# Input projections by Strassen's scheme in a two-layer transformer kernel: seven block products for eight, in two passes over halves of the contraction

## The chip, the cores and the metric

The kernel runs on one core of a Trainium2 chip. The core has a matrix engine (TensorE, PE in the profile; its weight loads are the row PEld), a vector engine (VectorE, DVE), an engine for activation functions (ScalarE, ACT), a general-purpose engine (GpSimd, POOL) and a queue engine that issues transfers (SyncE, SP). Each engine works through its own instructions in order and waits on semaphores. SBUF is the on-chip memory, PSUM the accumulators of the matmuls: eight banks of 128 x 512 fp32. The metric is the device time of one execution in microseconds; the time of a kernel is the median over its runs.

## The reference

Two layers of a mixer over 512 latent and 256 context tokens of width 2048. Cut to what matters:

```
for l in range(2):
    shift, scale, gate       = split(silu(c)     @ w_mod[l] + b_mod[l], 3)
    shift_c, scale_c, gate_c = split(silu(c_ctx) @ w_mod[l] + b_mod[l], 3)
    n  = rms_norm(h,  g)*(1 + scale)   + shift        # 512 x 2048
    nc = rms_norm(hc, g)*(1 + scale_c) + shift_c      # 256 x 2048
    p, pc = split(n @ w_in[l]), split(nc @ w_in[l])   # 2048 x 7168: 56 blocks of 128 columns
    # 16 heads of width 128 in four groups: A differential, B windowed with a sink,
    # C 2-D neighbourhood, D with normed q and k; latents also see the context's keys
    o  = attention(p, pc);  oc = attention of the context (layer 0 only)
    h  = h  + gate  * rms_norm((o  * silu(p[12]))  @ w_out[l], g2)
    hc = hc + gate_c* rms_norm((oc * silu(pc[12])) @ w_out[l], g2)   # layer 0 only
```

All is fp32. In layer 1 the context needs only keys and values.

## The kernel before

Every fp32 operand of a large matmul is split into a high part (rounded by ACT, `AF.Copy` into fp32r) and a low part (the rest, a subtraction on DVE): `split` (L175), where the rows L179 and L180 of the profile come from. A product is three matmuls, high by high, high by low and low by high: `mm3` (L185, rows L187 to L189).

The input projection treats one block of 128 output columns at a time (`proj_slots`, L565). The normed tokens lie in SBUF as 16 contraction tiles, split (`nh`, `nl` for the latents, `ch`, `cl` for the context). The weights of a block come as four chunks of four contraction tiles, 128 x 512 (`load_one`, L108); `weights_ahead` (L81) loads them, splits them into `wh`, `wl`, two ahead of their use. The weight tile is the stationary operand and the tokens stream, 512 latents and then, four slots later, 256 of the context (`ctx_steps`). A result is taken from its PSUM bank by the block's own function (`qk_block`, `v_block`, `g_block`).

The 16 heads are units in the order A, D, B, C. `plan` lists their blocks: key, value, query, gate (in B and D two heads share key and value). `layer` (L1061) writes the order out by hand: `drive` (L62) walks over the projection slots of one unit and puts in between, spread by weight, the steps of the previous heads (`head_steps`) and the steps of the modulation (`mod_steps`). A step of the softmax (`softmax_steps`, weight 1.5) multiplies queries by keys into the one score buffer (banks 3 and 4), DVE takes the maximum (L846, L876), ACT the exponential (L849, L886); POOL scales the row (L896). Then `value_steps` transposes, splits and multiplies by the values. Delayed pieces run some slots later (`later`, `tick`).

`mod_steps` (L298) works out shift, scale and gate: a 256 KB piece of `w_mod` is loaded, and DVE adds it, times a scalar, to one sum for the latents' condition and one for the context's (L327). Layer 1's shift and scale are made beside layer 0's projections. At the start of layer 0, `prologue` (L434) norms x and makes shift and scale, partly by matmuls (L479) and partly on DVE (L485), chunk by chunk beside the first unit's products. There POOL makes low parts (L100 for weights, L535 for tokens).

`out_phase` (L1114) multiplies by `w_out` in rounds of 512 output columns, first the context's, then the latents', with the last head's steps beside the first round. Between the layers, context products of layer 1 (`ctx_chunk`) run while the last residuals and norms are made.

The transposes of the heads are rows L917 and L784.

Of the kernel before, what the change touches and what calls it, by code (L numbers as in the profile page):

```python
# [10 lines left out]
F32 = mybir.dt.float32  # L11
# [25 lines left out]
GATE = 40  # L37


class Kernel:  # L40
# [37 lines left out]
    def weights_push(self, items):  # L78
        self.wq += items

    def weights_ahead(self):  # L81
        while self.wsplit < len(self.wq) and self.wsplit <= self.wpos + self.look:
            kind, key = self.wq[self.wsplit]
            if self.wsplit >= self.wload:
                if not self.load_one():
                    break
            raw = self.raws.pop(self.wsplit)
            if kind == "og":
                l, s, k = key
                w = raw.shape[1]  # L90
                hi = self.base.tile([P, w], F32R, tag=f"nh{s}_{k}", name=f"nh{s}_{k}")
                lo = self.base.tile([P, w], F32R, tag=f"nl{s}_{k}", name=f"nl{s}_{k}")
                self.og[s, k] = hi, lo
            else:
                hi = self.wp.tile([P, 512], F32R, tag="wh", bufs=4, name="wh")
                lo = self.wp.tile([P, 512], F32R, tag="wl", bufs=4, name="wl")
                self.ws[self.wsplit] = hi, lo
            if self.pool_lo and kind == "in":
                self.nc.scalar.activation(hi, raw, AF.Copy)  # L99
                self.nc.gpsimd.tensor_sub(lo, raw, hi.bitcast(F32))  # L100
            else:
                self.split(hi, lo, raw)
            self.wsplit += 1
        while self.wload < len(self.wq) and self.wload < self.wsplit + 3:
            if not self.load_one():
                break

    def load_one(self):  # L108
        nc, a = self.nc, self.a
        kind, key = self.wq[self.wload]  # L110
        if kind == "og" and key not in self.stored:
            return False
        raw = self.wp.tile([P, 512], F32, tag="wr", bufs=4, name="wr")
# [11 lines left out]
        self.raws[self.wload] = raw  # L125
# [3 lines left out]
    def weight(self):  # L129
        self.weights_ahead()  # L130
        while self.wq[self.wpos][0] == "og":
            self.wpos += 1
            self.weights_ahead()
        w = self.ws.pop(self.wpos)
        self.wpos += 1
        return w

# [16 lines left out]
    def split_to(self, dst, sl, src, scale=None):  # L154
        self.split(dst["h"][:, sl], dst["l"][:, sl], src, scale)
        dst["ready"] = dst.get("ready", 0) + sl.stop - sl.start

    def split_subs(self, dst, sl, src, scale=None):
# [3 lines left out]
        a, b = slice(0, 64), slice(64, P)  # L162
        if "d" not in dst:
            for t, r, o in ((dst["h"], a, b), (dst["l"], b, a)):
                A.activation(t[r, sl], src[r], AF.Copy)
                V.tensor_sub(t[o, sl], src[r], t[r, sl].bitcast(F32))
        else:
            for t, lo, r, o in ((dst["h"], dst["l"], a, b), (dst["d"], dst["m"], b, a)):
                A.activation(t[r, sl], src[r], AF.Copy, scale=scale)
                V.scalar_tensor_tensor(lo[r, sl], src[r], scale, t[r, sl].bitcast(F32), op0=ALU.mult, op1=ALU.subtract)  # L170
                A.activation(t[o, sl], src[r], AF.Copy, scale=scale)
                A.activation(lo[o, sl], lo[r, sl].bitcast(F32), AF.Copy)
        dst["ready"] = dst.get("ready", 0) + sl.stop - sl.start

    def split(self, hi, lo, src, scale=None):  # L175

        nc = self.nc
        if scale is None:
            nc.scalar.activation(hi, src, AF.Copy)  # L179
            nc.vector.tensor_sub(lo, src, hi.bitcast(F32))  # L180
# [4 lines left out]
    def mm3(self, out, lh, ll, rh, rl, start, stop):  # L185
        mm = self.nc.tensor.matmul
        mm(out, lh, rh, start=start, stop=False)  # L187
        mm(out, lh, rl, start=False, stop=False)  # L188
        mm(out, ll, rh, start=False, stop=stop)  # L189

    def run(self):
        tc, nc, a = self.tc, self.nc, self.a
        with ExitStack() as es:
            base = self.base = es.enter_context(tc.tile_pool(name="base", bufs=1))
            self.wp = es.enter_context(tc.tile_pool(name="wp", bufs=1))
            self.mp = es.enter_context(tc.tile_pool(name="mp", bufs=1))
# [5 lines left out]
            self.wq, self.raws, self.ws = [], {}, {}  # L202
            self.wpos = self.wsplit = self.wload = 0
            self.og, self.stored = {}, set()
            self.pool_lo = self.ctx_done = False
# [27 lines left out]
            self.ogd = self.dp.tile([DEPTH, KT, P, TOK], F32, name="ogd")  # L233
            self.plan()
            self.layer(0, self.prologue)

    def plan(self):

        self.units = []
        for h in range(4):  # L240
            self.units.append(("A", h, h, [("k", KA + h), ("v", VA + h), ("q", QA + h), ("g", GATE + h)]))
        for kind, q0, k0, v0, g0 in (("D", QD, KD, VD, 12), ("B", QB, KB, VB, 4)):
            for h in range(4):
                kv = [("k", k0 + h // 2), ("v", v0 + h // 2)] if h % 2 == 0 else []
                self.units.append((kind, h, g0 + h, kv + [("q", q0 + h), ("g", GATE + g0 + h)]))
        for h in range(4):
            self.units.append(("C", h, 8 + h, [("k", KC + h), ("v", VC + h), ("q", QC + h), ("g", GATE + 8 + h)]))
        self.order = [u[2] for u in self.units]
        for l in range(DEPTH):
            first = [b for _, b in self.units[0][3][:3]]  # L250
            if l > 0:
                for u in self.units[:2]:
                    for _, b in u[3][:2]:
                        self.weights_push([("in", (l, b, c)) for c in range(4)])
            self.weights_push([("in", (l, b, c)) for c in range(4) for b in first])
            for n, u in enumerate(self.units):
                for _, b in u[3][0 if n else 3:]:
                    self.weights_push([("in", (l, b, c)) for c in range(4)])
            for s in ((1, 0) if l < DEPTH - 1 else (0,)):
                for r in range(2 if s else 4):  # L260
                    for k in self.order:
                        if r == 0 and k != self.order[-1]:
                            self.weights_push([("og", (l, s, k))])
                        self.weights_push([("out", (l, k, c)) for c in ((2 * r, 2 * r + 1) if s else (r,))])


    def mod_columns(self, l, kind, c4, ps):
# [5 lines left out]
        if kind == 2:  # L273
# [7 lines left out]
            def turn():  # L281
                tp = self.tbank()[0:4 * ns, 0:P]
                nc.tensor.transpose(tp, t, self.ident)
                rows = self.x3()[0:4 * ns, 0:P]
# [13 lines left out]
    def mod_steps(self, jobs):  # L298
# [13 lines left out]
        def step(i):  # L312
# [22 lines left out]
    def mod_finish(self, job, accs, fold=True):  # L335
# [11 lines left out]
        if ns == 2:  # L347
            t, col = self.x3(), self.halves
# [69 lines left out]
    def make_n(self, l, stream, k, tiles, pool, t):  # L418

        nc = self.nc  # L420
        w = len(tiles) * P
        his, los = (self.nh, self.nl) if stream == 0 else (self.ch, self.cl)
        for i, ht in enumerate(tiles):
            nc.tensor.transpose(t[:, i * P:(i + 1) * P], ht[:, k * P:(k + 1) * P], self.ident)
        hi = self.base.tile([P, w], F32R, tag=f"nh{stream}_{k}", name=f"nh{stream}_{k}")
        lo = self.base.tile([P, w], F32R, tag=f"nl{stream}_{k}", name=f"nl{stream}_{k}")
        full = pool.tile([P, 512], F32, tag="full", bufs=2, name="full")[:, 0:w]
        mA, mB = self.mA[:, l, stream, k:k + 1], self.mB[:, l, stream, k:k + 1]
        nc.scalar.activation(hi, t[:, 0:w], AF.Identity, scale=mA, bias=mB)
        nc.vector.tensor_scalar(full, t[:, 0:w], mA, mB, op0=ALU.mult, op1=ALU.add)  # L430
        nc.vector.tensor_sub(lo, full, hi.bitcast(F32))
        his[k], los[k] = hi, lo

    def prologue(self, blocks):  # L434

        tc, nc, a = self.tc, self.nc, self.a
        self.nh, self.nl, self.ch, self.cl = ([None] * KT for _ in range(4))
        parts = ((0, SEQ), (SEQ, TOK))
        with tc.tile_pool(name="pro", bufs=1, reuse_waits="tile") as pool:
            raws, xs, accs = {}, [], {}  # L440
            seq = [(c4, kind, kk) for c4 in range(4) for kk in range(8) for kind in (1, 0)]
            self.np = 0

            def load(upto):
                while self.np < min(upto, len(seq)):
                    c4, kind, kk = seq[self.np]
                    raw = raws[seq[self.np]] = pool.tile([P, 2, 512], F32, tag="mr", bufs=8, name="mr")
                    col0 = kind * D + c4 * 512
                    nc.sync.dma_start(raw, a["w_mod"][0, kk * 256:(kk + 1) * 256, col0:col0 + 512].rearrange("(k p) c -> p k c", p=P))
                    self.np += 1  # L450

            def load_x(upto):
                while len(xs) < upto:
                    t = pool.tile([P, TOK], F32, tag="x", bufs=KT, name="x")
                    nc.sync.dma_start(t, a["xt"][len(xs)])
                    xs.append(t)

            load(2)
            load_x(KT)
            load(8)  # L460
            tot = [self.mp.tile([P, 512], F32, tag="macc", bufs=2, name="tot")[:, 0:w1 - w0] for w0, w1 in parts]

            def squares(k):
                for t, (w0, w1) in zip(tot, parts):
                    if k == 0:
                        nc.scalar.activation(t, xs[k][:, w0:w1], AF.Square)
                        continue
                    sq = self.mp.tile([P, 512], F32, tag="mraw", bufs=3, name="sq")[:, 0:w1 - w0]
# [911 lines left out]
```

## Time and profile before

| | |
|---|---|
| median of 3 runs (lowest, highest) | 2792.03 us (2788.14, 2792.82) |
| profiled execution: time, span | 2796.49 us, 2794.7 us |
| PE, PEld busy | 2693.9 us (96%), 2234.6 us (80%) |
| DVE, ACT, POOL busy | 1751.9 us (63%), 1045.1 us (37%), 313.2 us (11%) |
| moved by DMA | 331.24 MB, mean 119 GB/s |
| granted clock of TensorE, mean | 0.986 |

A row of the profile's groups reads: line, engine, operation, output <- inputs, shapes, count | busy us, mean ns of one | idle time before it and what ended it. PE counts matmuls as busy from issue to the modelled end, so overlapped ones have durations that add up to more than their time.

### The profile page before, as it was taken

What the parts mean: (1) busy time and instruction counts of PE and PEld (TensorE: products, weight loads), DVE (VectorE), ACT (ScalarE), POOL (GpSimd) and SP (SyncE); (2) the same over time, 40 slices, a digit from 0 to 9 for tenths busy, and PEclk for the clock granted to TensorE, in tenths of its full rate; (3) what the DMA queues carried; (4) which work ended last, traced back from release to release, by engine and by line L of the source; (5) the groups of instructions that cost most, each with busy time, mean ns of one, the idle gap of its engine ahead of it and who ended that gap; (6) DMA issues with size and microseconds to landing.
All of it is one profiled execution on the core that took longest, in us unless ns stands there. A gap on an engine that the chain in (4) does not pass through costs nothing. (4 is left out here: it accounts for less than half of the span.)

```text
span 2794.7 us, 38989 instructions
## 1 busy us (share of the span) xinstructions
PE 2693.9 (96%) x14348; PEld 2234.6 (80%) x14348; DVE 1751.9 (63%) x3399; ACT 1045.1 (37%) x2087; POOL 313.2 (11%) x266
## 2 busy tenths in 40 slices
PE   6989999999999999999999989999999999999997
PEld 1468888888888888888778777888888788888885
DVE  6886988876974746664564577666755644334524
ACT  3334444433333333333553255444433333333422
POOL 1530000011111101010010030000001111000001
PEclk8999999999999999999999989999999999999998
DMA  8841323232431414443763542112312322222533
GB/s 313 279 136 61 119 82 115 86 121 75 152 116 59 125 59 128 126 129 93 222 219 113 184 164 87 61 61 95 111 58 68 128 71 76 81 81 89 177 113 106
DMA packets 178642, 331.24 MB, mean 119 GB/s; under 512 B 20833, under 2 KB 24209, under 8 KB 177937
## 3 DMA queue, kind: packets, MB, share of 16 engines
q1 hardware_dynamic: 178448, 328.74, 36.5%
q8 instruction: 112, 1.84, 0.3%
q14 instruction: 82, 0.66, 0.1%
HBM read 310.42 MB, written 18.24 MB: 118 GB/s over the span
## 5 line engine op out<-in xcount | busy, mean ns | idle before, releaser
L187 PE MATMUL ps<-nh,wh 128*128 128x512 f32 (+1 forms) x3072 | 1079.2, 352 | 11.1 <-ACT wh L99 7.9
L188 PE MATMUL ps<-nl,wh 128*128 128x512 f32 (+1 forms) x3072 | 1065.8, 347 | 5.3 <-POOL nl L535 5.2
L189 PE MATMUL ps<-nh,wl 128*128 128x512 f32 (+1 forms) x3072 | 1066.1, 347 | 4.6 <-POOL wl L100 4.6
L180 DVE TENSOR_TENSOR wl<-wr,wh 128x512 fp32r<-128x512 f32 x624 | 450.0, 723 | 554.9 <-ACT wh L179 537.6
L179 ACT ACTIVATE wh<-wr 128x512 fp32r<-128x512 f32 x624 | 392.7, 630 | 905.2 <-PE ps L188 478.3
L187 PEld LDWEIGHTS ps<-nh,wh 128*128 128x128 f32 x3072 | 582.0, 190 | 92.0 <-issue 10.0
L189 PEld LDWEIGHTS ps<-nh,wl 128*128 128x128 f32 x3072 | 580.7, 189 | 80.4 <-POOL wl L100 6.1
L188 PEld LDWEIGHTS ps<-nl,wh 128*128 128x128 f32 x3072 | 582.0, 189 | 73.8 <-POOL nl L535 9.3
L327 DVE SCALAR_TENSOR_TENSOR macc<-mraw,sc,macc 128x512 f32<-128x512 f32 x420 | 309.8, 771 | 50.4 <-DMA mraw<-in_w_mod 49.9
L188 PE MATMUL ps<-wl,nh 128*128 128x512 f32 x600 | 239.5, 399 | 6.0 <-DVE wl L180 5.9
L187 PE MATMUL ps<-wh,nh 128*128 128x512 f32 x600 | 238.5, 398 | 0.1
L189 PE MATMUL ps<-wh,nl 128*128 128x512 f32 x600 | 238.2, 397 | 0.0
L180 DVE TENSOR_TENSOR PTl<-ps,PTh 128x512 fp32r<-128x512 f32 (+2 forms) x224 | 132.6, 592 | 108.7 <-ACT PTh L179 108.4
L896 POOL TENSOR_SCALAR P<-P,small 128x768 f32<-128x768 f32 (+2 forms) x96 | 97.5, 1015 | 835.7 <-DVE small L895 742.4
L179 ACT ACTIVATE PTh<-ps 128x512 fp32r<-128x512 f32 (+2 forms) x224 | 115.8, 518 | 162.4 <-PE ps L917 155.8
L650 POOL TENSOR_TENSOR rt<-rt 128x512 f32<-128x512 f32 x40 | 62.1, 1552 | 967.8 <-DVE rt L647 967.8
L188 PEld LDWEIGHTS ps<-wl,nh 128*128 128x128 f32 x600 | 113.3, 189 | 36.7 <-DVE wl L180 10.5
L187 PEld LDWEIGHTS ps<-wh,nh 128*128 128x128 f32 x600 | 113.3, 189 | 27.8 <-ACT wh L179 1.0
L189 PEld LDWEIGHTS ps<-wh,nl 128*128 128x128 f32 x600 | 113.5, 189 | 27.0
L917 PE MATMUL ps<-ident,P 128*128 128x128 f32 x672 | 105.2, 272 | 1.4 <-DVE PTl L180 1.3
L917 PEld LDWEIGHTS ps<-ident,P 128*128 128x128 f32 x672 | 83.5, 140 | 24.1 <-DVE PTl L180 1.8
L876 DVE TENSOR_REDUCE small<-ps 128x1 f32<-128x768 f32 (+3 forms) x120 | 88.8, 740 | 11.4 <-PE ps L189 7.4
(232 smaller groups left out, 2882.6 us busy)
## 6 DMA issues: line engine op xcount, KB each, us to landing
wr<-in_w_in SPq DMA_DIRECT2D x464, 256.0 KB, 3.0
mraw<-in_w_mod SPq DMA_DIRECT2D x256, 256.0 KB, 3.0
wr<-in_w_out SPq DMA_DIRECT2D x192, 256.0 KB, 3.3
mr<-in_w_mod SPq DMA_DIRECT2D x64, 512.0 KB, 5.3
wr<-ogd SPq DMA_DIRECT2D x30, 256.0 KB, 2.7
x<-in_xt SPq DMA_DIRECT2D x16, 384.0 KB, 7.8
ogd<-g SPq DMA_DIRECT2D x15, 384.0 KB, 2.7
h<-in_x SPq DMA_DIRECT2D x16, 256.0 KB, 4.9
```

Of the source, the lines that this page charges most:

```text
L179: nc.scalar.activation(hi, src, AF.Copy)
L180: nc.vector.tensor_sub(lo, src, hi.bitcast(F32))
L187: mm(out, lh, rh, start=start, stop=False)
L188: mm(out, lh, rl, start=False, stop=False)
L189: mm(out, ll, rh, start=False, stop=stop)
L327: nc.vector.scalar_tensor_tensor(acc, raw, col, acc, op0=ALU.mult, op1=ALU.add)
L650: nc.gpsimd.tensor_add(t1, t1, t2)
L876: nc.vector.reduce_max(nm, sv, axis=AX, negate=True)
L896: nc.gpsimd.tensor_scalar(Pt, Pt, sm, 0.5, op0=ALU.mult, op1=ALU.mult)
L917: nc.tensor.transpose(T[:, i * P:(i + 1) * P], st["P", t][:, c:c + P], self.ident)
```

## The change

Two blocks make a pair: (key, value) or (query, gate). Tokens are kept in two halves of 384 (256 latents and 128 of the context each). A pass takes half of the contraction, 8 of the 16 tiles, again in two halves of four. So a pass is a 2 x 2 by 2 x 2 block product, and Winograd's form of Strassen's scheme makes it from seven products, numbered 1 to 7, in the order 1, 6, 2, 5, 7, 3, 4, accumulated in three PSUM banks (`CHAIN`).

- Weights: POOL forms the sums s1 and s2 and two differences of a pair's four chunks in each pass (`sums`, `split_product`), then ACT and DVE split seven operands. In the second pass the low parts for products 5 and 7 are made by POOL.
- Tokens: the seven token operands of a pass, split, stay in one area of SBUF (`arena`); `reload` writes them for the first pair of a pass, or after the last pair of the pass before. The output phase keeps its gated heads in the same area.
- Results: ACT copies product 1 out of PSUM; the others are added to it by DVE as they end. The first pass writes the sums of all 56 blocks to DRAM (`part`), the second one fetches them a pair ahead (`hold_parts`), POOL adds product 1 to three quarters of them, and DVE the rest.
- Order: a layer is now first pass over all 28 pairs, with only modulation and the second half's token work beside it, and then the second pass over all 28 pairs, with all heads' steps beside it, at a density set by `goal`. The block functions read the result from SBUF, not from PSUM.
- Layer 0's prologue makes only the first halves of shift and scale, by matmuls, before the first pair. The rest and the gate (128 steps) run beside the first pass. Layer 1's shift and scale (128 steps) run beside the latents' rounds of layer 0's output phase; its gate (64 steps, one stream) beside its first pass.
- In `mod_steps` the context's stream is made by ACT (product) and POOL (sum) and not by DVE.
- The context products between the layers (`ctx_chunk`) go; the context's normed tokens pass through DRAM (`cnd`).

```
+    def sums(self, g):
+        if g["sums"] or not all(self.need(g, i) for i in range(3)):
+            return g["sums"]
+        add = self.nc.gpsimd
...
+        add.tensor_add(g["s1"], g[1], g[2])
+        add.tensor_sub(g["s2"], g["s1"], g[0])
+        add.tensor_sub(g[1], g[0], g[1])
...
+    def split_product(self, g, n):
...
+        src = {1: 0, 6: "s2", 2: 3, 5: "s1", 7: 1, 3: 3, 4: 2}[n]
+        hi, lo = self.new_pair()
+        self.split(hi, lo, g[src], pool=n in self.pool_lo)
+        if n == 2:
+            self.nc.gpsimd.tensor_sub(g[3], g[3], g["s2"])
...
             for acc, s in zip(accs[j], streams):
                 col = self.sc[:, k, s:s + 1]
+                if s == 1:
+                    t = acc if k == 0 else self.mp.tile([P, 512], F32, tag="mt", bufs=2, name="mt")
+                    nc.scalar.activation(t, raw, AF.Copy, scale=col)
+                    if k:
+                        nc.gpsimd.tensor_add(acc, acc, t)
+                    continue
...
+    def pair_slots(self, l, s, n, i, hooks=None):
...
+        def slot(m, half):
+            if half == 0:
+                for fn in before.get(m, ()):
+                    fn()
+                r["w"] = self.weight()
+            hi, lo = r["w"]
+            th, tl = self.operand(m)
+            out = self.bank(CHAIN[m], w)
+            for j in (2 * half, 2 * half + 1):
+                js = slice(j * P, (j + 1) * P)
+                self.mm3(out, hi[:, js], lo[:, js], th[:, j, 0:w], tl[:, j, 0:w], m in FIRST and j == 0, m in LAST and j == 3, True)
+            if half:
+                read(m, out)
...
+        def read(m, ps):
+            V = nc.vector
+            if m == 1:
+                r["c"] = tiles()
...
+                nc.scalar.activation(r["s"], ps, AF.Copy)
+                if s:
+                    for c, h in ((r["c"][1], 0), (r["c"][1], 1), (r["c"][0], 1)):
+                        nc.gpsimd.tensor_add(c[:, h], c[:, h], r["s"])
...
+                c = {6: c2[:, 0], 4: c2[:, 0], 5: c2[:, 1], 7: c2[:, 1], 3: c1[:, 1]}[m]
+                V.tensor_add(c, ps, c if s or m in (7, 4) else s1)
...
+                    nc.sync.dma_start(self.part[l, b, :, :, 0:w], c)
...
+        self.drive(slots[0])
...
+        self.drive([x for s in slots[1:-1] for x in s], self.late)
+        self.drive(slots[-1])
...
+        self.pool_lo = (5, 7)
+        steps, left, last = [], 0, 0
+        for n, (kind, h, gh, prs) in enumerate(self.units):
...
+            goal = left - last * (0 if n == len(self.units) - 1 else 0.3 if len(prs) > 1 else 0.7)
...
+            self.drive([x for i in range(len(prs)) for x in self.pair_slots(l, 1, n, i)], now)
```

A query/gate pair of layer 1 has only the latents, 256 a half.

More of the change, by code (lines that the diff above doesn't have):

```diff
@@ L98, in weights_ahead @@
[L98 to L102, printed above, removed]
+            kind, g, key = self.wq[self.wsplit]
+            if not (self.split_product(g, key) if kind == "st" else self.split_one(kind, g, key)):
+                break
             self.wsplit += 1
-        while self.wload < len(self.wq) and self.wload < self.wsplit + 3:
+        while self.load_one():
+            pass
@@ new lines, in reload, with step, reloads @@
+    def reload(self, n, ns, ts, pool=()):
+        hi, lo = self.operand(n)
+        def step(j):
+            if n in (1, 2, 3):
+                src = ns[j + (0 if n == 1 else 4)][:, int(n == 3)]
+            else:
+                src = ts[j][{5: 0, 7: 0, 6: 1, 4: 1}[n]]
+            self.split(hi[:, j], lo[:, j], src, pool=j in pool)
+        return [lambda j=j: step(j) for j in range(4)]
+    def reloads(self, ns, ts, pool=()):
+        out = {n: self.reload(n, ns, ts, pool) for n in ORDER}
+        out[6] += self.token_sums(ns, ts, 4, True)
+        out[5] += self.token_sums(ns, ts, 3, True)
+        return out
@@ L629, in x3, with hold_parts @@
+    def hold_parts(self):
+        if not self.to_hold:
+            return
+        l, blocks, w = self.to_hold.pop(0)
+        out = []
+        for _, b in blocks:
+            c = self.cp.tile([P, 2, HT], F32, tag="c", bufs=4, name="c")[:, :, 0:w]
+            self.nc.sync.dma_start(c, self.part[l, b, :, :, 0:w])
+            out.append(c)
+        self.held.append(out)
     def x3(self):
@@ L1057, in unit_blocks, with layer @@
             else:
-                out.append(self.g_block(l, b, dst))
-        return out
-    def layer(self, l, start):
+                fn = self.g_block(l, b, dst)
+            self.take[n, what] = fn
+    def layer(self, l):
         tc, nc, a = self.tc, self.nc, self.a
-        sts = {}
-        blocks = {n: self.unit_blocks(l, n, sts) for n in range(len(self.units))}
-        start(blocks[0])
+        pairs = [(n, i) for n, u in enumerate(self.units) for i in range(len(u[3]))]
+        self.tbanks, self.tb = [5, 6], 0
+        before = {m: self.first[ORDER[i + 1]] if i + 1 < len(ORDER) else [] for i, m in enumerate(ORDER)}
+        before[ORDER[0]] = self.first[ORDER[0]] + before[ORDER[0]]
+        again = self.reloads(self.ns2, self.ts2)
+        slots = []
+        for p in pairs:
+            hooks = (before, {}) if p == pairs[0] else ({}, again) if p == pairs[-1] else None
+            slots.append(self.pair_slots(l, 0, *p, hooks))
+        self.drive(slots[0])
@@ L1107, in layer @@
-        self.ctx_steps()
-        self.pend = None
+        self.take, sts = {}, {}
+        for n in range(len(self.units)):
+            self.unit_blocks(l, n, sts)
+        self.held = []
+        self.to_hold = []
+        for n, i in pairs:
+            blocks = self.units[n][3][i]
+            wide = l < DEPTH - 1 or blocks[0][0] == "k"
+            self.to_hold.append((l, blocks, HT if wide else 2 * P))
+        self.hold_parts()
+        self.pool_lo = (5, 7)
+        steps, left, last = [], 0, 0
```

745 lines of the change are left out of this document (386 added, 359 removed).

## The prediction

> **What bounds the kernel now.** I read the totals on the page first, then the chain that ended last, then the groups of instructions by shape, then single rows in order of time.
>
> ```profile
> span 2794.7 us, 38989 instructions
> PE 2693.9 (96%) x14348; PEld 2234.6 (80%) x14348; DVE 1751.9 (63%) x3399; ACT 1045.1 (37%) x2087; POOL 313.2 (11%) x266
> PE   6989999999999999999999989999999999999997
> PE 34%; DVE 2%; ACT 1%; DMA 0%; issue 0%; POOL 0%; DVEq 0%; POOLq 0%
> ```
>
> TensorE works through the whole span but for the start, the seam between the layers and the end, and it leads the chain of waits. Its busy time counts overlapped matmuls, so the price of one is taken from the distance between starts:
>
> ```profile
> 872.82 0.34 PE L188 MATMUL ps<-PTl,vh 128*128 128x384 f32 x1
> 873.00 0.34 PE L189 MATMUL ps<-PTh,vl 128*128 128x384 f32 x1
> ...
> 1141.76 0.39 PE L187 MATMUL ps<-nh,wh 128*128 128x512 f32 x1
> 1141.99 0.39 PE L188 MATMUL ps<-nl,wh 128*128 128x512 f32 x1
> ...
> 1142.56 0.28 PE L188 MATMUL ps<-nl,wh 128*128 128x256 f32 x1
> 1142.68 0.28 PE L189 MATMUL ps<-nh,wl 128*128 128x256 f32 x1
> ```
>
> A 512-wide matmul takes 0.2325 us (mean over a longer run of such starts; 0.23 here), a 256-wide 0.118, a 384-wide 0.1745. The counts:
>
> ```profile
> L187 PE MATMUL ps<-nh,wh 128*128 128x512 f32 x1792 | 717.7, 401 | 2.0 <-ACT wh L99 1.6 <-DVE mB L292 0.4
> L187 PE MATMUL ps<-nh,wh 128*128 128x256 f32 x1280 | 362.6, 283 | 9.1 <-ACT wh L99 6.3 <-DVE kl L166 2.9
> L187 PE MATMUL ps<-wh,nh 128*128 128x512 f32 x600 | 238.5, 398 | 0.1
> L917 PE MATMUL ps<-ident,P 128*128 128x128 f32 x672 | 105.2, 272 | 1.4 <-DVE PTl L180 1.3
> L187 PE MATMUL ps<-PTh,vh 128*128 128x512 f32 x128 | 59.7, 466 | 0.0
> L187 PE MATMUL ps<-kh,qh 128*128 128x256 f32 x152 | 43.7, 287 | 0.8 <-ACT Pc L886 0.6 <-ACT P L886 0.2
> ```
>
> Each row stands three times (L187, L188, L189). Projections: 3 × (1792 × 0.2325 + 1280 × 0.118) = 1703 us, 61% of the span. Output: 1920 (with 40 on the last head's tiles) × 0.2325 = 446. Attention, by the same widths and all its counts, about 396: 208 in layer 0, 188 in layer 1.
>
> **The change, term by term.** *Matmuls.* A pair of output blocks costs 7 products × 4 contraction tiles × 3 = 84 matmuls in each of two passes, 384 wide, or 256 wide for the 16 query/gate pairs of layer 1: 40 × 168 × 0.1745 + 16 × 168 × 0.118 = 1490. TensorE sheds 213 us. One wide pair in one pass is then 14.7 us, a narrow one 9.9.
>
> *What is paid for it.* Weight tiles to split go from 8 to 14 a pair; POOL forms four sums of 128x512 a pair and pass, all of SBUF operands; five or six reads of PSUM a pair and pass replace one or two; layer 0's second stream of the modulation moves from DVE to ACT and a POOL add; all heads move into the second pass; layer 1's modulation moves from layer 0's projections to its output phase. Prices:
>
> ```profile
> L327 DVE SCALAR_TENSOR_TENSOR macc<-mraw,sc,macc 128x512 f32<-128x512 f32 x420 | 309.8, 771 | 50.4 <-DMA mraw<-in_w_mod 49.9
> L180 DVE TENSOR_TENSOR wl<-wr,wh 128x512 fp32r<-128x512 f32 x624 | 450.0, 723 | 554.9 <-ACT wh L179 537.6 <-PE ps L917 5.6 <-PE ps L784 4.6
> L180 DVE TENSOR_TENSOR PTl<-ps,PTh 128x384 fp32r<-128x384 f32 x32 | 17.7, 554 | 11.9 <-ACT PTh L179 11.9
> 118.00 5.82 POOL L100 TENSOR_TENSOR wl<-wr,wh 128x512 fp32r<-128x512 f32 x1 [6.47 <-ACT wh L99]
> 119.29 3.39 DVE L485 SCALAR_TENSOR_TENSOR macc<-mr,sc,macc 128x512 f32<-128x512 f32 x5
> 126.24 1.27 POOL L100 TENSOR_TENSOR wl<-wr,wh 128x512 fp32r<-128x512 f32 x1 [2.42 <-ACT wh L99]
> 171.50 5.73 POOL L535 TENSOR_TENSOR nl<-x,nh 128x256 fp32r<-128x256 f32 x4
> 172.01 5.77 DVE L327 SCALAR_TENSOR_TENSOR macc<-mraw,sc,macc 128x512 f32<-128x512 f32 x4
> ```
>
> The last five rows matter most. DVE alone runs five 512-wide operations in 3.39 us, 0.66 each; a POOL subtraction that takes 1.27 alone lasted 5.82 while DVE did so. Where both are queued, four DVE and four POOL operations (two 512 wide, two 256) take 5.7 us, not the 2.7 of DVE alone: they take turns. Four times 0.66 from 5.73 leaves 3.09 for POOL, so 1.03 for a 512-wide one. DVE and POOL operations with two SBUF operands add up, 1.69 us for one of each. The subtraction from PSUM keeps its price beside POOL, so only the SBUF ones count.
>
> The Trainium skill (SBUF — State Buffer, Who interferes with whom) says that a DVE instruction with two SBUF inputs and a GpSimd instruction that reads SBUF block each other, the second until the first has finished. With POOL's whole 1.27 a turn would cost 1.93, and the 256 turns below 61 us more than in my sum; the trace agrees on the blocking, and its 1.69 a turn is used.
>
> *By stage* (span of the profiled execution, 2794.7 us; its time is 2796.5, 4.5 above the median of the three runs):
>
> ```profile
> mr<-in_w_mod SPq DMA_DIRECT2D x64, 512.0 KB, 5.3
> 0.00:100.00 100.00, 75.87 (x227) 27.84 (x228) 74.46 (x135) 35.81 (x71) 24.18 (x21) 0.88 0.87 304
> 300.00:600.00 300.00, 296.12 (x1759) 256.57 (x1758) 255.95 (x578) 121.85 (x254) 20.26 (x13) 1.00 0.35 108
> 1000.00:1200.00 200.00, 200.00 (x1212) 177.70 (x1212) 116.51 (x220) 65.22 (x138) 21.63 (x24) 1.00 0.35 109
> 1610.00:1630.00 20.00, 16.25 (x98) 14.54 (x97) 16.85 (x33) 12.29 (x32) 8.87 (x7) 0.84 0.63 221
> 1800.00:2200.00 400.00, 395.79 (x2120) 335.42 (x2119) 246.32 (x504) 155.36 (x287) 31.61 (x27) 1.00 0.25 80
> ```
>
> (These are windows: PE, PEld, DVE, ACT, POOL busy, granted clock, DMA share, GB/s.)
>
> 1. Start: only the first halves of scale and shift (16.8 MB, 32 of the 512 KB loads) and x (6.3 MB) stand ahead of the first product: 77 us at 304 GB/s, 23 for what cannot overlap (statistics before the first matmuls, modulation, operand splits). 100.
> 2. Layer 0, first pass: TensorE needs 28 × 14.7 = 410. The shared turn needs 28 × (4 × 1.03 + 7 × 0.66) = 245 for weights and 128 modulation steps × 1.69 = 216: 461. DVE's stalls hold its weight splits, those hold TensorE. 480 (ends: 425, if turns hide; 540, if the PSUM reads never overlap POOL).
> 3. Hand-over of operands, twice: 28 splits on ACT and DVE in one pair's time: 10 each (0 to 20).
> 4. Layer 0, second pass: matmuls 410 + 208 = 618. Some 394 weighted head steps now fall into 392 slots of six matmuls (1.05 us), twice as dense as before. One buffer holds the scores, so the next scores wait for this chain:
>
> ```profile
> 1850.30 0.40 PE L822 MATMUL ps<-kh,qh 128*128 128x512 f32 x1
> 1851.21 0.96 DVE L846 TENSOR_REDUCE small<-ps 128x1 f32<-128x768 f32 x1 [1.00 <-PE ps L823]
> 1852.21 0.90 ACT L849 ACTIVATE P<-ps,small 128x768 f32<-128x768 f32 x1 [2.83 <-DVE small L846]
> L886 ACT ACTIVATE P<-ps,small,rs 128x768 f32<-128x768 f32 x32 | 31.7, 990 | 46.7 <-DVE small L883 42.3 <-DVE rs L400 2.6 <-PE ps L189 1.9
> L876 DVE TENSOR_REDUCE small<-ps 128x1 f32<-128x640 f32 x32 | 26.3, 820 | 2.1
> ```
>
> 2.81 us from the first score to the end of the exponential in group A, by the other rows about 3.5 in D and 3.0 to 3.5 in B and C. Available are 1.4 slots (1.45 us) plus the scores' own 0.7 to 1.06: 2.05 to 2.5. The difference over 32 + 16 + 32 latent steps is 65 us. Before, the slots of these steps took over 3 us, which is why windows like 1000 to 1200 show no idle time. Waiting behind other DVE work is not in that row (0.01 us there); before, DVE was 58 to 85% busy with most of it, now its own work is about 83% (of its 1752 us, 310 and 450 are the modulation and weight rows above, some 430 of the rest layer 0's heads; 28 pairs × (5 × 0.66 + 6 × 0.5) = 176 more; 606 of 728), with POOL's turns on top: between 0 and 1 us a step, 0.4 taken, 45 for 120 steps. 728.
> 5. Output of layer 0: context rounds 384 × 0.2325 = 89, plus the 16 of idle time they have now. Latent rounds: matmuls 179, but 128 × 1.69 for the modulation, 64 + 15 + 8 operations of 0.66: 273; 280 taken. Sum 385.
> 6. Seam: the row at 1610 shows it; now nothing fills the tail (15 us for residual and second norm), then 8 × 1.3 us on ACT for the new operands, the first splits and a cooled clock: 40. Before, 20 us of context products lay there.
> 7. Layer 1, first pass: 12 × 14.7 + 16 × 9.9 = 335; a narrow pair also needs 8.7 of shared turns and 1.5 of modulation, just over its 9.9. 345 (335 to 365).
> 8. Layer 1, second pass: 335 + 188 = 523, chain 44 by the same comparison, 30 for DVE waits (80 steps × 0.4). 597.
> 9. Output of layer 1: 768 × 0.2325 = 179 and the 24 of today's tail. 203.
>
> Sum: 100 + 480 + 20 + 728 + 385 + 40 + 345 + 597 + 203 = 2898, 101 above the profiled execution's time with its 1.8 us around the span; 2893 against the median, rounded to **2890**. In short: 213 us of matmuls and some 70 of today's start and small stalls are won, and spent on turns (70 + 101), stalls in dense heads (184) and hand-overs. The sums in DRAM go by SP's queue:
>
> ```profile
> DMA packets 178642, 331.24 MB, mean 119 GB/s; under 512 B 20833, under 2 KB 24209, under 8 KB 177937
> wr<-in_w_in SPq DMA_DIRECT2D x464, 256.0 KB, 3.0
> ```
>
> 22 MB written and read again in layer 0, less in layer 1, beside 331 MB at 119 GB/s where the start shows 304: costed at nothing, covered by their being fetched one pair (14.7 us) ahead; uncovered, 3.0 us of landing a pair, 84 a layer.
>
> **Rivals.** *Faster: turns and waits hide.* If a modulation step costs under (410 − 245) / 128 = 1.3 us of shared time, pass one is bound by matmuls, and under 1.0 the output rounds are too: then 55 and 95 us go, with half the DVE waits 2705. For it: 50 to 60% use of each engine. Against: the rows at 171 us. If the softmax chains hid too, 2560, which needs a second score buffer that isn't there.
> *Slower still: POOL late.* In second passes POOL makes the low parts for products 5 and 7. POOL stands in order behind the scaling of P, which waits for a reciprocal that stands on DVE behind the next step's maximum. What queues behind: the low parts and the next pair's sums, needed two products (4.2 us, narrow 2.8) later. 2 us lost a pair is 112: 3005. Turns that hold POOL's whole 1.27 would end on the way there, 2950, and share this chance; the four and four in 5.7 us speak against it. That length is what the Trainium skill's section named above would make of it.
> *No change:* with the smallest of my terms (no DVE waits, 461 and 273 bare, no hand-over, 335, a seam of 33) the sum is 2760; DVE waits of 0.1 us a step and half the hand-overs bring it to 2790, where gain and losses meet.
>
> **How the numbers follow.** Forecast 0.48, POOL late 0.15, no change 0.05, turns hide 0.26, all hides 0.06. Slower by over 0.2% (what a measurement here can tell) 0.63, same 0.05, faster 0.32. The likeliest case alone spans 2810 to 2960; the range 2670 to 3000 leaves out full hiding and the upper half of POOL late.
>
> **What would show it.** Right: in layer 0's first pass DVE operations with two SBUF operands over 1.2 us beside a POOL busy above 60%; idle TensorE waiting for `wl`; in second passes TensorE waiting on ACT P; latent output rounds over 250 us. Wrong: 384-wide products back to back at 0.175 us through pass one, DVE durations of 0.7 beside POOL, output rounds near 185.

## The result: 19% slower, where 3.5% was forecast

The changed kernel takes 3314.01 us (median of 4 runs, 3310.43 to 3314.50) against 2792.16: ratio 1.187, 95% interval 1.1849 to 1.189. The direction was forecast, the size was not: 522 us lost for 98, and the time lies 314 above the end of the range. The profiled execution took 3314.17 us. From the page of the changed kernel: totals, the DVE, POOL and clock lines of the 40 slices; and from its view of cores:

```profile
span 3312.4 us, 43903 instructions
PE 2728.5 (82%) x14488; PEld 2415.7 (73%) x14488; DVE 2583.7 (78%) x4076; ACT 1484.5 (45%) x2900; POOL 1652.1 (50%) x1230
DVE  4988769889989877766898987788788788776634
POOL 0776547664335455551366645543554355566301
PEclk8788898989888999999998869999889898989999
...
core 0: 3312.4 us, clock 0.905
```

TensorE was 96% busy before and is 82% now; no engine is near full over the whole span, so they wait for each other. The granted clock fell from 0.986 to 0.905. The stages, as windows (PE, PEld, DVE, ACT, POOL busy, granted clock, DMA share, GB/s): layer 0's first pass, its second, its output with the seam, layer 1's first pass, its second.

```profile
91.20:684.30 593.10, 473.33 (x2427) 454.66 (x2426) 492.71 (x562) 273.80 (x473) 389.77 (x257) 0.89 0.44 143
684.30:1513.20 828.90, 703.01 (x3798) 633.78 (x3797) 676.19 (x1321) 379.05 (x829) 421.38 (x347) 0.92 0.24 76
1513.20:1951.40 438.20, 326.71 (x1350) 254.12 (x1348) 378.49 (x503) 237.23 (x451) 210.54 (x141) 0.86 0.66 209
1951.40:2357.80 406.40, 369.27 (x2431) 361.73 (x2430) 324.64 (x437) 173.49 (x324) 202.77 (x137) 0.94 0.47 154
2357.80:3105.00 747.20, 601.76 (x3511) 545.47 (x3510) 579.90 (x1022) 327.78 (x657) 403.89 (x327) 0.90 0.24 76
```

Set against the forecast, with the distances between the starts of all matmuls in the trace split into three: what the matmul takes at full clock, what it takes more without waiting (half clock), and waits. The split rests on how a lengthened distance is assigned; other rules give 190 to 240 us of half clock and 660 to 710 of waits.

| stage | forecast | measured | full clock | half clock | waits |
|---|---|---|---|---|---|
| start | 100 | 91 | 58 | 2 | 24 |
| layer 0, first pass | 480 | 593 | 419 | 38 | 136 |
| layer 0, second pass, hand-over | 738 | 829 | 616 | 58 | 155 |
| output 0 and seam | 425 | 438 | 291 | 27 | 120 |
| layer 1, first pass | 345 | 406 | 341 | 21 | 44 |
| layer 1, second pass, hand-over | 607 | 747 | 505 | 71 | 171 |
| output 1 | 203 | 207 | 187 | 1 | 2 |
| sum | 2898 | 3312 | 2417 | 218 | 652 |

(The other 25 us lie ahead of the first matmul and behind the last.)

What TensorE waited for, over the whole span (total us, times, longest):

```profile
PE ps L284 <- DVE c L762: 123.6, 63, 5.7
PE ps L460 <- DVE fold L455: 66.3, 6, 29.6
PE ps L1071 <- POOL P L1050: 47.8, 23, 5.2
PE ps L284 <- ACT s L750: 46.1, 14, 7.4
PE ps L285 <- DVE PTl L276: 41.6, 27, 5.4
...
PE ps L976 <- ACT P L1003: 23.1, 16, 3.5
PE ps L285 <- DVE wl L276: 22.4, 13, 7.6
PE ps L284 <- ACT P L1040: 18.2, 22, 2.7
...
PE ps L286 <- DVE wl L276: 13.1, 9, 4.0
PE ps L286 <- POOL wl L276: 11.9, 4, 4.2
```

The largest wait is for the reads of PSUM (`c`, 124 us), not for weight splits (`wl`, 47 in three rows). The groups of the first pass of layer 0 (busy us, mean ns, idle before):

```profile
L429 DVE SCALAR_TENSOR_TENSOR macc<-mraw,sc,macc 128x512 f32<-128x512 f32 x120 | 155.1, 1292 | 3.0 <-DMA mraw<-in_w_mod 1.7
L276 DVE TENSOR_TENSOR wl<-wr,wh 128x512 fp32r<-128x512 f32 x139 | 151.4, 1091 | 41.3 <-ACT wh L275 41.0 <-PE ps L286 0.2
L762 DVE TENSOR_TENSOR c<-ps,s 128x384 f32<-128x384 f32 x84 | 46.2, 550 | 22.4 <-PE ps L286 22.2
...
L424 POOL TENSOR_TENSOR macc<-macc,mt 128x512 f32<-128x512 f32 x120 | 185.4, 1545 | 93.2 <-ACT mt L422 85.6 <-ACT macc L422 4.4 <-DMA mraw<-in_w_mod 0.8
...
L422 ACT ACTIVATE mt<-mraw,sc 128x512 f32<-128x512 f32 x120 | 86.6, 723 | 149.0 <-POOL macc L424 125.7 <-DMA mraw<-in_w_mod 21.2 <-PE ps L460 1.6
```

A read of PSUM itself kept its 0.55 us. What made it late is what stands ahead of it in DVE's order, as rows of the timeline show (start, us, operation):

```profile
568.78 6.67 POOL L424 TENSOR_TENSOR macc<-macc,mt 128x512 f32<-128x512 f32 x4
569.18 1.77 DVE L276 TENSOR_TENSOR wl<-wr,wh 128x512 fp32r<-128x512 f32 x1
570.45 0.72 ACT L422 ACTIVATE mt<-mraw,sc 128x512 f32<-128x512 f32 x1 [0.75 <-POOL macc L424]
570.87 0.54 DVE L762 TENSOR_TENSOR c<-ps,s 128x384 f32<-128x384 f32 x1
...
571.56 0.41 PE L284 MATMUL ps<-arena,wh 128*128 128x384 f32 x1 [1.61 <-DVE c L762]
...
572.55 1.78 DVE L429 SCALAR_TENSOR_TENSOR macc<-mraw,sc,macc 128x512 f32<-128x512 f32 x1
...
575.93 0.68 DVE L276 TENSOR_TENSOR wl<-s,wh 128x512 fp32r<-128x512 f32 x1
```

Beside POOL, DVE's operations take 1.77 and 1.78 us; a split of the same shape once POOL is done, at 575.93, takes 0.68. The read of PSUM stands behind the first of them, and the matmul at 571.56 has waited 1.61 us for it.

### The profile page after: what moved, and what is told of

The parts are those of the page before. It is cut to its first block, busy times and chain, and to the rows that moved or that the text cites. A ratio compares the mean times of both kernels' runs of the same rounds, so it can differ in the third digit from the quotient of the medians.

```text
span 3312.4 us, 43903 instructions
## 1 busy us (share of the span) xinstructions
PE 2728.5 (82%) x14488; PEld 2415.7 (73%) x14488; DVE 2583.7 (78%) x4076; ACT 1484.5 (45%) x2900; POOL 1652.1 (50%) x1230
## 5 line engine op out<-in xcount | busy, mean ns | idle before, releaser
L284 PE MATMUL ps<-arena,wh 128*128 128x384 f32 (+1 forms) x3136 | 1078.9, 344 | 181.0 <-DVE c L762 123.1
L286 PE MATMUL ps<-arena,wl 128*128 128x384 f32 (+1 forms) x3136 | 1058.0, 338 | 25.2 <-DVE wl L276 13.1
L285 PE MATMUL ps<-arena,wh 128*128 128x384 f32 (+1 forms) x3136 | 1060.7, 338 | 10.4 <-POOL arena L276 6.0
L276 DVE TENSOR_TENSOR wl<-wr,wh 128x512 fp32r<-128x512 f32 x696 | 629.5, 908 | 209.1 <-ACT wh L275 198.6
L284 PEld LDWEIGHTS ps<-arena,wh 128*128 128x128 f32 x3136 | 634.8, 202 | 212.0 <-DVE c L762 92.2
L286 PEld LDWEIGHTS ps<-arena,wl 128*128 128x128 f32 x3136 | 634.1, 202 | 32.2 <-DVE wl L276 16.6
L285 PEld LDWEIGHTS ps<-arena,wh 128*128 128x128 f32 x3136 | 635.3, 203 | 18.3 <-POOL arena L276 9.1
L424 POOL TENSOR_TENSOR macc<-macc,mt 128x512 f32<-128x512 f32 x240 | 373.3, 1556 | 267.8 <-ACT mt L422 243.2
L762 DVE TENSOR_TENSOR c<-ps,c 128x384 f32<-128x384 f32 (+1 forms) x392 | 201.2, 514 | 136.8 <-PE ps L286 83.1
L285 PE MATMUL ps<-wl,arena 128*128 128x512 f32 x640 | 261.3, 408 | 22.7 <-DVE wl L276 22.4
L284 PE MATMUL ps<-wh,arena 128*128 128x512 f32 x640 | 260.9, 408 | 3.1 <-ACT cn L526 2.3
L286 PE MATMUL ps<-wh,arena 128*128 128x512 f32 x640 | 259.0, 405 | 0.0
L149 POOL TENSOR_TENSOR s<-wr 128x512 f32<-128x512 f32 x112 | 174.2, 1555 | 80.7 <-DMA wr<-in_w_in 57.7
```

The lines of the kernel that those rows point to most:

```text
L149: add.tensor_add(g["s1"], g[1], g[2])
L276: (nc.gpsimd if pool else nc.vector).tensor_sub(lo, src, hi.bitcast(F32))
L284: mm(out, lh, rh, start=start, stop=False, skip_group_check=parts)
L285: mm(out, lh, rl, start=False, stop=False, skip_group_check=parts)
L286: mm(out, ll, rh, start=False, stop=stop, skip_group_check=parts)
L424: nc.gpsimd.tensor_add(acc, acc, t)
```

## The experiments

### What each part of POOL's new work costs

Theory: POOL's operations slow DVE, and through DVE's, ACT's and TensorE's orders the whole. So each kind was moved to DVE, alone and then all together. The modulation's second stream (the branch with ACT's product and POOL's addition is never taken, so both streams are made by DVE):

```
-                if s == 1:
+                if False:
```

> The changed kernel with both streams of the modulation on DVE again; POOL keeps the weight sums, the low parts of products 5 and 7 and the additions of the first pass's sums. Theory (POOL's share of the modulation takes turns with DVE, ACT waits for POOL with weight splits queued behind it, and TensorE falls to half clock): layer 0's first pass falls from 593 us to 430-490, output and seam of layer 0 from 438 to about 385, the second passes stay within 20 us; total 3060 to 3180. Rival (DVE is simply full, and POOL's share relieves it): 128 operations of 0.66 us come to DVE in each of the two places, total 3350 to 3480.

3214.72 us, ratio 1.1516 (1.1498 to 1.1533): 99 less than the changed kernel. The direction fits, the size is under the theory's: layer 0's first pass fell to 538, not to 430 to 490, which leaves more to the other kinds. The weight sums:

```
-        add = self.nc.gpsimd
+        add = self.nc.vector
-            self.nc.gpsimd.tensor_sub(g[3], g[3], g["s2"])
+            self.nc.vector.tensor_sub(g[3], g[3], g["s2"])
```

> The changed kernel, with only the four weight sums and differences of a pair (128x512, SBUF operands) on DVE instead of POOL: 56 pairs and passes, 224 operations. The modulation's second stream, the additions of first parts and the low parts of products 5 and 7 stay on POOL. Moving the modulation alone won 99 us and moving all of POOL's new work 374. Theory (every POOL operation on SBUF holds up the DVE operations beside it and through them TensorE, so each kind counts by its number): 120 to 200 us faster than the changed kernel's 3314, 3115 to 3195, with something won in each of the four passes. Rival (what counts is only where POOL stands in order in the second passes): under 60 us, all but none of it in the first passes.

3115.63 us, ratio 1.1148 (1.1124 to 1.1172): 198 less, at the fast end of the theory, with something won in all four passes. (The operations are 448, 56 pairs in two passes by four; 224 was a miscount.) The first parts and the low parts:

```
-                        nc.gpsimd.tensor_add(c[:, h], c[:, h], r["s"])
+                        nc.vector.tensor_add(c[:, h], c[:, h], r["s"])
-        self.pool_lo = (5, 7)
+        self.pool_lo = ()
```

> The changed kernel, with the additions of the first parts (three of 128x384 or 128x256 a pair, second passes only) and the low parts of products 5 and 7 on DVE instead of POOL; the weight sums and the modulation's second stream stay on POOL. With the heads left out the second passes still waited 215 us for DVE's reads of PSUM, which need what POOL added. Rival of the prediction, POOL late: the second passes shrink by 110 us or more together (829 to under 770, 747 to under 695) and nothing else moves; 3140 to 3200. Theory that every POOL operation counts by its number: 168 additions and 56 low parts, the same count as the weight sums and in a shorter time, 80 to 150 us, also only in the second passes; so this run and the one with the sums on DVE should add up, with the modulation's 99, to about the 374 of all three. If they add to much less, the parts cover for each other.

3200.41 us, ratio 1.146 (1.1442 to 1.1477): 114 less, nearly all in the second passes, 53 in each. (The operations are 280: 168 additions and 112 low parts, not 56.) That lies inside the theory and just short of what the rival asked for, and both put it into the second passes, so the run does not tell them apart. The trace of the changed kernel shows how much is lateness alone: DVE waited 51 us for POOL's additions to the parts, TensorE 12 for POOL's low parts. The three edits together:

> The changed kernel with all that POOL was given on DVE: both modulation streams, the four weight sums of a pair and pass, the low parts of products 5 and 7, the additions of the first pass's sums. POOL is left with what it did before. Theory (taking turns costs more than the work itself): DVE alone needs 16.3 us a pair in layer 0's first pass: 460 to 480 us there, second passes 750 to 800 and 660 to 700, total 2990 to 3150. Rival (DVE load is what counts): every stage gets longer than in the changed kernel, total above 3400.

2940.25 us, ratio 1.0534 (1.0515 to 1.0554): 374 less, faster than expected. The parts add to 411, so they overlap by 37. Moving an operation takes away three things at once: what it adds to DVE's operations beside it, the waits for POOL itself, and in the modulation a product on ACT. Stages, in us:

| stage | changed | modulation | sums | parts | all |
|---|---|---|---|---|---|
| layer 0, first pass | 593 | 538 | 544 | 590 | 470 |
| layer 0, second pass | 829 | 827 | 777 | 776 | 754 |
| output 0 and seam | 438 | 393 | 431 | 440 | 395 |
| layer 1, first pass | 406 | 406 | 376 | 405 | 377 |
| layer 1, second pass | 747 | 750 | 691 | 694 | 646 |

The page's totals with all on DVE, and four of its groups:

```profile
PE 2608.4 (89%) x14488; PEld 2306.3 (79%) x14488; DVE 2553.8 (87%) x5060; ACT 1325.7 (45%) x2644; POOL 299.4 (10%) x262
...
L276 DVE TENSOR_TENSOR wl<-wr,wh 128x512 fp32r<-128x512 f32 x752 | 531.3, 708 | 139.1 <-ACT wh L275 135.5
L429 DVE SCALAR_TENSOR_TENSOR macc<-mraw,sc,macc 128x512 f32<-128x512 f32 x540 | 390.2, 757 | 21.0 <-DMA mraw<-in_w_mod 20.3
...
L149 DVE TENSOR_TENSOR s<-wr 128x512 f32<-128x512 f32 x112 | 76.5, 683 | 3.9 <-issue 1.3 <-DMA lt<-in_lam 1.3 <-DMA wr<-in_w_in 0.9
...
L753 DVE TENSOR_TENSOR c<-c,s 128x384 f32<-128x384 f32 x120 | 71.1, 630 | 0.3
```

The most telling pair of numbers: DVE took over 984 operations (4076 to 5060), and its busy time fell, from 2583.7 to 2553.8 us. What POOL had relieved DVE of had come back in full as longer DVE operations.

### The same move in the kernel before

The kernel before with the context's modulation stream as ACT product and POOL addition:

```
+                if s == 1:
+                    t = acc if k == 0 else raw
+                    nc.scalar.activation(t, raw, AF.Copy, scale=col)
+                    if k:
+                        nc.gpsimd.tensor_add(acc, acc, t)
+                    continue
```

> The kernel before with one part of the change alone: the context's modulation stream is scaled by ACT (in place in the loaded piece) and summed by POOL, 192 steps in layer 0's projections and none elsewhere. Theory: DVE sheds 127 us there, but 192 turns of 1.03 us come in; where TensorE had slack it costs little: 2800 to 2880. Rival (POOL's work beside DVE is free): DVE is relieved and the time stays at 2785 to 2795.

2880.44 us, ratio 1.0317 (1.03 to 1.0334), the theory's upper end: 88 us lost by this move alone, in a kernel with no Strassen and room on DVE. Its 192 products on ACT are part of the move: ACT waited 117 us for DVE to be done with the piece that it scales in place, and TensorE's waits for the exponentials grew from 11 to 38 us. How the 88 divide was not tested.

### Is it ACT's place behind POOL?

The same in two places, cut to the argument that changes:

```
-  tag="mt", bufs=2
+  tag="mt", bufs=3 if self.mp is self.ph else 2
```

> The changed kernel with three buffers instead of two for the modulation's product that ACT makes and POOL adds, in layer 0's stage only (there is no room for it in the output phase). In the first pass of layer 0 ACT waited 126 us for POOL to free such a buffer, with the copies of weights for TensorE behind it in its order, while DVE was idle a sixth of the time. Theory (the pass is long because ACT stands behind POOL, and not because the turns fill it): the pass falls from 593 by 20 to 60 us, and ACT's wait for POOL by half; 3255 to 3295. Rival (the turns set the rate: POOL and DVE share one port, a deeper buffer only moves where the waiting is): the pass stays within 10 us of 593; 3304 to 3324.

3300.42 us, ratio 1.1828 (1.1808 to 1.1848). The pass shrank by 11 us, between the two expectations. ACT's wait for POOL fell from 126 to 89, TensorE's for ACT `s` from 39 to 25, but its wait for DVE `c` rose from 67 to 75. ACT's place is a small part; mostly the waiting moved.

### Dense heads, or the second pass itself?

The changed kernel without scores, softmax and values (each head keeps only its last step):

> The changed kernel without scores, softmax and values: a head ends right after its projections and the gate alone is stored, so the attention is left out. Theory (the heads beside the second pass are too dense for DVE and POOL in order): the second passes fall from 829 and 747 us to about 480 and 390, near the 410 and 335 of their matmuls; total about 2610. Rival (the second pass is slow by itself, by POOL's additions and low parts): they stay above 600 and 520, total above 2860. First passes and output unchanged under both.

2868.61 us in one run, as the rival said. Its two second passes:

```profile
683.00:1284.20 601.20, 482.98 (x2506) 462.43 (x2505) 475.55 (x682) 227.63 (x440) 374.52 (x272) 0.91 0.30 100
2110.20:2670.10 559.90, 419.49 (x2492) 405.38 (x2491) 424.34 (x606) 209.90 (x390) 359.12 (x274) 0.87 0.29 97
```

They still took 601 and 560 us, though their matmuls at full clock are 428 and 349: 173 and 211 lost with no head in them, 202 of it waits of TensorE for DVE `c`. The theory that dense heads cause the loss fell. With heads, the passes take 228 and 187 more, of which 188 and 156 are matmuls: dense heads cost 40 + 31 us beyond their matmuls. The same with all of POOL's new work on DVE:

> The kernel with all of POOL's new work on DVE, and the heads' scores, softmax and values left out (finish alone stays), so the second passes hold the projections, their parts and what the heads leave to set up. With POOL burdened the same passes without heads took 601 and 560 us, against 428 and 349 of matmuls. Theory (POOL's work is what slows the second pass by itself): 430 to 480 and 350 to 400, the whole 2500 to 2600. Rival (a second pass waits because a part is needed two products after it is fetched, whoever adds it): over 560 and over 500.

2451.33 us in one run, and windows of its two second passes:

```profile
559.60:1057.50 497.90, 450.88 (x2507) 437.86 (x2506) 470.87 (x936) 234.07 (x446) 35.68 (x25) 0.96 0.37 121
1798.40:2252.90 454.50, 388.63 (x2491) 375.88 (x2490) 434.89 (x854) 211.18 (x387) 36.92 (x26) 0.93 0.37 118
```

498 and 455, both over the theory's 430 to 480 and 350 to 400; the first lies far under the rival's 560, the second halfway between 400 and the rival's 500. (The total, 2451, is under the theory's 2500 to 2600.) POOL's work accounts for 103 and 105 us of the passes. For the rest, DVE is 95% and 96% busy and never waits for a part to arrive, which speaks for DVE as the bound and against the rival. With POOL's work on DVE, heads add 256 and 191 us (754 and 646 with them), 68 + 35 beyond their matmuls.

### Turns and pauses by themselves

A measurement apart from the kernel: runs of 24 operations of 128x512, and bursts of matmuls with pauses.

> Not the kernel but a measurement of two disputed costs; it computes nothing of the reference. First, 24 operations of 128x512 each: DVE on two SBUF operands alone (about 0.66 us each by the prediction's row), POOL alone (1.27), then both at once, then POOL beside DVE reading one PSUM operand, beside DVE with one SBUF operand and a column, POOL with one operand beside DVE with two, POOL beside ACT, and POOL beside DVE alternating two SBUF operands and PSUM. The prediction's turn: both at once take 1.69 us for one of each; a turn that holds POOL's whole operation would take 1.93; no coupling 1.27. PSUM reads, one-operand DVE and ACT keep their times beside POOL by the prediction, and there POOL keeps 1.27. Second, TensorE in bursts with pauses for a copy on ACT: 8 matmuls of 512 (1.9 us at full clock) with pauses of about 0.4, 0.7, 1.2 and 2.4 us, then 40 (9.3 us) with pauses of about 2.4 and 4.5. Theory from the changed kernel's records (a stretch of 3.41 us in which TensorE is used less than about 40% is followed by one at half clock): full clock at the first two, mixed at the third, half clock at most of the fourth, one or two half stretches a pause in the last. Rival (only a whole idle stretch of 3.41 us halves it): full clock in the first five, some half clock in the last.

Its groups: DVE alone (L42), POOL alone (L45), both on two SBUF operands (L48, L49), DVE from PSUM beside POOL (L56, L57), DVE with one operand and a column beside POOL (L60).

```profile
L42 DVE TENSOR_TENSOR d<-w,w 128x512 f32<-128x512 f32 x24 | 17.1, 711 | 0.8
L45 POOL TENSOR_TENSOR g<-w,w 128x512 f32<-128x512 f32 x24 | 30.7, 1277 | 2.1 <-DVE d L39 0.3
L48 DVE TENSOR_TENSOR d<-w,w 128x512 f32<-128x512 f32 x24 | 38.7, 1613 | 0.8
L49 POOL TENSOR_TENSOR g<-w,w 128x512 f32<-128x512 f32 x24 | 38.8, 1616 | 2.1 <-DVE d L39 0.3
L56 DVE TENSOR_TENSOR c<-ps,w 128x512 f32<-128x512 f32 x24 | 16.6, 690 | 0.7
L57 POOL TENSOR_TENSOR g<-w,w 128x512 f32<-128x512 f32 x24 | 30.6, 1275 | 2.2 <-DVE d L39 0.4
L60 DVE TENSOR_SCALAR d<-w,col 128x512 f32<-128x512 f32 x24 | 33.3, 1389 | 0.8
```

One operation of each takes 1.61 us, near the prediction's 1.69; DVE alone does two in 1.42. Sharing such work with POOL is slower than not sharing it. PSUM reads are free of it, as forecast (690 ns beside POOL, 690 alone), and so is ACT (629, 634 alone). One-operand DVE operations are not, against the forecast: 1389. A POOL operation on one operand still holds DVE, 877 for 711. Where DVE alternates two SBUF operands with PSUM, its two-operand operations still take 1353. The Trainium skill (SBUF — State Buffer, Who interferes with whom) has DVE with two SBUF inputs and GpSimd block each other in full; that would be 0.71 + 1.28 = 1.99, and the 1.61 is less: the two overlap in part.

Windows over five bursts of 40 matmuls with pauses of 3.02 us (from the last matmul's start to the next one's), and six with pauses of 5.53:

```profile
429.00:497.00 68.00, 54.86 (x200) 42.88 (x200) 0.00 (x0) 11.94 (x20) 0.00 (x0) 0.87 0.00 0
526.70:628.00 101.30, 75.54 (x260) 59.26 (x260) 0.00 (x0) 23.88 (x40) 0.00 (x0) 0.81 0.00 0
```

Each pause of 3.02 us is followed by one stretch of 3.41 us at half clock, each of 5.53 by two. Bursts of 8 with pauses of 0.8 and 1.1 us kept full clock. All pauses came out longer than expected; at 1.8 and 3.3 us other waits stood between the small bursts and the clock was mixed. The rival, a whole idle stretch of 3.41, falls at 3.02. But these bursts repeat every 13.6 and 17.0 us, four and five stretches, so every pause lies at the same place against the stretches: each row is one case repeated, not five or six.

### What follows, tried

If POOL never wins against DVE, it should do nothing in either kernel. All POOL arithmetic of the kernel before on DVE (seven places, as this one), then the same in the changed kernel:

```
-            nc.gpsimd.tensor_add(t1, t1, t2)
+            nc.vector.tensor_add(t1, t1, t2)
```

> The kernel before the change with all of POOL's arithmetic (264 operations, 313 us of POOL) on DVE. If POOL's operations on SBUF cost by holding DVE even in a kernel that TensorE bounds, DVE's mean times fall (723 to about 690 for the weight splits, 771 to about 755 for the modulation) and the start, where POOL and DVE worked side by side, shortens: theory 2760 to 2792, 0 to 1% faster. Rival (the work was hidden where TensorE has no idle time, and DVE now stands in the softmax chains in its place): 2785 to 2830.

> The changed kernel with all of POOL's arithmetic on DVE: its new work, as in the run of 2940 us, and what it did before the change (299 us: the scaling of P, the rotations' additions, the operands' sums and splits). DVE was busy 87% of that run and POOL's remaining operations waited for it. Theory (POOL never wins against DVE, an operation of each takes 1.61 where DVE alone does two in 1.42): 2900 to 2945. Rival (DVE is now the bound, and the scaling of P adds to its queue in the second passes): 2945 to 3040.

The kernel before: 2746.5 us (5 runs), ratio 0.9839 (0.9823 to 0.9855), 1.6% faster than the kernel before and past the theory's end. The changed kernel: 2928.7, ratio 1.0486 (1.047 to 1.0502), inside the theory, 12 less than with 299 us left on POOL. From the page and the groups of the first:

```profile
PE 2675.2 (98%) x14348; PEld 2226.4 (81%) x14348; DVE 1781.4 (65%) x3661; ACT 1046.4 (38%) x2087; POOL 0.2 (0%) x4
...
L180 DVE TENSOR_TENSOR wl<-wr,wh 128x512 fp32r<-128x512 f32 x624 | 429.4, 690 | 510.4 <-ACT wh L179 493.3 <-PE ps L784 4.6 <-PE ps L917 3.9
L896 DVE TENSOR_SCALAR P<-P,small 128x768 f32<-128x768 f32 x32 | 19.8, 619 | 0.7
```

DVE took over 313 us of POOL and is busy 30 us longer. The same share of all matmuls is started 22 us sooner by 5%, 29 by half, 45 by 60%, 55 by 70%, and the span ends 56 sooner. So the gain falls at the start, at the seam between the layers and just behind it; where TensorE fills the time, there is little. Two causes are not separated there: longer DVE operations, and POOL's own time (a 512-wide weight split took POOL 1.73 us at the start, now DVE 0.69).

## Why the prediction missed

**Right.** The matmuls: 419 us at full clock in the first pass for 410; pairs with no modulation beside them ran in 14.6 and 9.9 us, as forecast. The turn's price, PSUM reads that keep theirs, the start, the output phases, and the sums in DRAM, for which TensorE shows no wait. Of the signs named, two-operand DVE operations of 1.29 and 1.09 us beside a POOL busy 66% came, and latent output rounds of 275 us. Waits for `wl` stayed small, and so did those for ACT P in the second passes (41 us). Two sums are off by 1 and 2 us (23.1 MB at 304 GB/s are 76; 2898 adds up spans, so it is 103 above 2794.7); neither matters.

**Step 2 (480, measured 593): a turn's price was right, its use was not.** The 461 us of turns were summed as if DVE and POOL were one machine that is never idle and on which nothing else stands. DVE was busy 493, with 77 us of PSUM reads (139 of 0.55) and the operands' splits and folds inside, and idle for 100 more: 46 for ACT's `wh`, 42 for products. The upper end, 540, had the reads but no waits and no half clock.

**Steps 4 and 8 (738 and 607 with the hand-overs, measured 829 and 747): the step that failed most.** The turns that step 2 priced were left out here, and the loss was put on the heads. POOL's four sums, three part additions and two low parts a pair stood only in the 0.4 us a head step for all DVE waits, 45 us in layer 0. At the prediction's own 1.03 us for a 512-wide one they come, as an estimate, to 28 x (6 x 1.03 + 3 x 0.77), some 240 us, beside its 606 of DVE work in 728. Measured: with POOL's new work on DVE the two passes take 754 and 646, so that work costs 75 + 101 us. Taken singly, the sums cost 52 + 56 and the parts 53 + 53. Of the 184 us forecast for chains and DVE waits of dense heads, 71 came in the changed kernel, 103 with POOL's new work on DVE.

The rival "POOL late", low parts and sums that stand behind the scaling of P, was priced at 112. The low parts and part additions cost 106 there, the sums 108, so the near size is in part luck. Lateness itself shows in the trace with 51 us of DVE's waits for POOL's additions, 12 of TensorE's for POOL's low parts and 48 for the scaled P (15 once POOL has only its old work). And it had a chance of 0.15 as an alternative, when it came on top.

**Step 7 (345, measured 406)** had the turns, 10.2 us a narrow pair against 9.9 of matmuls, and missed as step 2 did; with the sums on DVE the pass takes 376.

**Steps 5 and 6 (425, measured 438)** came close: context rounds 110 for 105, latent rounds 275 for 280, with DVE busy 91% in them as a bound by turns asks for, and a seam of 54 for 40. The form of the wait had no term: matmuls of the modulation stood up to 29.6 us in TensorE's order for a DVE addition (`fold`, 66 us in all). Whether the stage would be shorter without that wait alone was not tested.

**Hardly in the sum: the clock.** It was assumed at full speed behind every stall but the seam's. Some 218 us are matmuls at half clock, some 121 with POOL's new work on DVE; a part of every other loss is this second price. In these runs it fell with the waits.

**What stays.** With POOL empty the change still loses 136 us, and 182 against the kernel before with POOL empty too. DVE is then the likely bound: with only POOL's new work moved it was busy 464 of 470 us in layer 0's first pass, and 85 to 94% in the stages behind. The 213 us of matmuls are paid for with 14 weight tiles to split, sums and reads on an engine that had the modulation already. No run makes DVE's work lighter to prove it. How the 37 us of overlap between the three parts divide, and what the 1.61 us turn consists of, was not settled.

## What to carry to other kernels

Before work is put on an idle POOL, take one pair of operations from the trace where DVE and POOL ran together: if one of each takes longer than two on DVE, as here for two fp32 operands in SBUF, the idle engine is no resource for them, and emptying it can be the gain. When an engine's operations get longer, price what stands behind them in its order, not only the operations. And price a stall of TensorE with the half clock behind it: here some 650 us of waits brought some 220 more.

## What the runs showed of the hardware

- One-operand operations are not safe beside POOL: DVE with a tile and a column took 1389 ns there, 482 alone (the modulation's first steps in the kernel before with POOL empty).
- The clock is set in stretches of 3.41 us. In the changed kernel's records, a stretch in which TensorE worked under 35% of the time (its matmuls counted at their price by width) was followed by one at half clock 102 times of 102; at 35 to 55%, 39 of 80; above, 30 of 753. The Trainium skill (TensorE: Matmul & The Clock Gate, Part 1) gives the 3413 ns and says that at least one idle one brings half clock. The length agrees; a stretch that is two thirds idle was enough here.
